# Tap products of a Hyena filter: high and low fp32r parts stacked on the summed index, two passes each, in place of whole fp32 factors

## The chip, the cores and the metric

The kernel runs on one core of one Trainium2 chip. The metric is the device time of the whole program in microseconds (us), where less is better. A time of the chip is the median of several runs; the profile is of one further execution, with its own time.

## The reference

The program is one layer of an encoder with two mixers side by side, run on a sample of 1024 positions and on a prompt of 256 positions. One mixer is grouped attention with rotary positions, the other is a Hyena operator: a long convolution whose filter a small network computes from the position. After them come an output projection, a gated feed-forward part and a final norm. What matters here is the filter:

```python
h = jnp.sin(fr * (z @ w1 + b1))          # (L, 64)
h = jnp.sin(fr * (h @ w2 + b2))          # (L, 64)
h = (h @ w3).reshape(L, N_DIRS, HY_WIDTH)   # (L, 2, 512): the taps
h = h * jnp.exp(-t[:, :, None] * jnp.abs(decay)[None])
...
return k / jnp.sum(jnp.abs(k), axis=0, keepdims=True)
```

`z` holds 33 position features and the hidden width is 64, so the product with `w3` sums over 64 terms. It is taken for both sequence lengths, forward and backward, over 512 channels.

## The kernel before

The program is written with a tile framework: pools hand out buffers by tag (a tag has a fixed number of slots), and the order of the instructions on each engine comes from a list scheduler that simulates the program while it is built, with its own estimates of the durations. Inside one engine the instructions run in that order.

The first part of the program projects the normed input onto the Hyena columns (`proj_hy`). It has 12 column tiles; each loads a 1024x128 weight block, splits it into an fp32r high part `wh` (a cast on ACT, line 498) and a low part `wl` (a subtraction on POOL, line 159), and multiplies it with the split input `ah`/`al`, three fp32r passes for each term (`mm3`, lines 166 to 168: high by high, low by high, high by low). The trace calls these products `us` (512 columns wide) and `up` (256 wide). ACT and DVE then apply a short convolution to the result `u`. The weight parts sit in the tag `w4`, which has 8 slots of 4 KB for each partition.

Interleaved with it runs `filter_stream`. It computes the two sine layers for 512 and 128 columns; the upper 64 partitions hold the second half of the positions, the lower 64 the first half. The results are `h2s` (in tag `s2`, 8 slots) for the sample and `h2p` (tag `s1`) for the prompt. Then `taps_of` runs four times, for the prompt's two halves of 256 channels (P0, P1) and the sample's two (S0, S1). It loads `w3` twice, into the lower and the upper partitions, and multiplies one 64-row slice of `h2` (128 positions) with the matching 64 rows of `w3` (512 columns: 256 channels in two directions) at line 352. There are 2 such products in each prompt half and 8 in each sample half. DVE multiplies each with an exponential from ACT (`h`, line 355), ACT and POOL gather the sums of magnitudes (`acc`), and DVE forms sums and differences (`e`, `q`). From these, further DVE work (`C`, `gaf`, `gtf`) and transform products (`fx`, line 281) make the filter's spectrum, which goes to DRAM. After the filter the main stream goes on with the query columns (`proj_att`), whose weights use `w4` too.

In the trace the tile names lose their digits: `f` is the tap product, `w` is `w3`. Line 159 is a helper that issues every elementwise two-input operation.

Of the kernel before, what the change touches and what calls it, by code (L numbers as in the profile page):

```python
# [12 lines left out]
F32R = mybir.dt.float32r  # L13
# [24 lines left out]
MUL, ADD, SUB = ALU.mult, ALU.add, ALU.subtract  # L38
# [62 lines left out]
def hymba_layer_kernel(ctx: ExitStack, tc: tile.TileContext, A, dbg=None):  # L101
    nc = tc.nc
    dbg = dbg or {}
    V, S, G, T, Q = nc.vector, nc.scalar, nc.gpsimd, nc.tensor, nc.sync
# [16 lines left out]
    def pool(tag, bufs, of=None):  # L121
        def make(name, shape, dt=F32):
            return (of or mem).tile([128] + list(shape), dt, name=name, tag=tag, bufs=bufs)
        return make


    w4, pf, u5 = pool("w4", 8), pool("pf", 10, res), pool("u5", 3)
    s2, r2, s1, fh = pool("s2", 8, mid), pool("r2", 3, mid), pool("s1", 5), pool("fh", 2, mid)
# [7 lines left out]
    def b1(name):  # L136
        return psm.tile([128, 512], F32, name=name, tag="b1", bufs=1)
# [11 lines left out]
    def bh(name):  # L149
        return psm.tile([128, 512], F32, name=name, tag="bh", bufs=2)  # L150

    def flat(t):
        return t.rearrange("p a b -> p (a b)")

    def stt(out, in0, scalar, in1, op0=MUL, op1=ADD, eng=None):
        (eng or V).scalar_tensor_tensor(out=out, in0=in0, scalar=scalar, in1=in1, op0=op0, op1=op1)

    def tt(out, in0, in1, op, eng=None):
        return (eng or V).tensor_tensor(out=out, in0=in0, in1=in1, op=op)  # L159

    def f(ap):
        return ap.bitcast(F32)
# [122 lines left out]
    def filter_stream():  # L285
# [11 lines left out]
        def sin_layer(ps, n, b, out):  # L297
            a = s2("sa", [512])[:, 0:n]
            V.tensor_scalar(out=a, in0=ps, scalar1=cols[:, b:b + 1], scalar2=cols[:, 58:59], op0=ADD, op1=MUL)
            k = s2("sk", [512])[:, 0:n]  # L300
            V.tensor_scalar(out=k, in0=a, scalar1=1.0 / (2 * math.pi), scalar2=MAGIC, op0=MUL, op1=ADD)
            V.tensor_scalar(out=k, in0=k, scalar1=MAGIC, scalar2=None, op0=SUB)
            for cw in CW:
                stt(a, k, -cw, a)
            V.tensor_scalar(out=a, in0=a, scalar1=PI_LO, scalar2=-PI_LO, op0=ALU.min, op1=ALU.max)
            S.activation(out=out, in_=a, func=AF.Sin)

        h2s = s2("h2s", [512])
        h2p = s1("h2p", [128])
        for n, off, h2 in ((512, 0, h2s), (128, 512, h2p)):  # L310
            p = b1("fp")
            T.matmul(out=p[:, 0:n], lhsT=w1bd, rhs=zf[0:66, off:off + n], start=True, stop=True)
            h1 = s2("h1", [512])[:, 0:n]
            with tc.issue_after(held[0].ins):
                sin_layer(p[:, 0:n], n, 56, h1)
            p = b1("fq")
            T.matmul(out=p[:, 0:n], lhsT=w2bd, rhs=h1, start=True, stop=True)
            sin_layer(p[:, 0:n], n, 57, h2)
            yield

        def taps_of(seq, hf, out):

            h2, na, toff = (h2s, 8, 0) if seq == "S" else (h2p, 2, 8)
            si = 0 if seq == "S" else 1
            nm = f"{seq}{hf}"
            cs = slice(hf * 256, (hf + 1) * 256)
            w3 = fh("w3", [2, 256])
            absd = fh("absd", [2, 256])
            for d in range(2):
                for h in range(2):  # L330
                    Q.dma_start(out=w3[h * 64:(h + 1) * 64, d],
                                in_=A["hy_f_w3"][0][:, d * HY + hf * 256:d * HY + (hf + 1) * 256])
                Q.dma_start(out=absd[:, d], in_=A["hy_decay"][0, d:d + 1, cs].broadcast_to([128, 256]))
            S.activation(out=absd, in_=absd, func=AF.Abs)
            acc = s2(f"acc{nm}", [512])
            if seq == "S":
                e, q = [], []
            else:
                e = [s2(f"e{nm}", [2, 256])]
                q = [s2(f"q{nm}", [2, 256])]  # L340
            half = na // 2
            for a2 in range(half):
                if seq == "S" and a2 % 2 == 0:
                    e.append(pf(f"e{a2 // 2}{nm}", [4, 256]))
                    q.append(pf(f"q{a2 // 2}{nm}", [4, 256]))
                h = pf(f"h{nm}", [2, 512])
                for i in range(2):
                    a = 2 * a2 + i
                    up = a >= half
                    p = bh("f3")  # L350
                    hs = slice(64, 128) if up else slice(0, 64)
                    T.matmul(out=p, lhsT=h2[hs, (a % half) * 128:(a % half) * 128 + 128],
                             rhs=flat(w3[hs]), start=True, stop=True)
                    S.activation(out=h[:, i], in_=flat(absd), func=AF.Exp, scale=negt[:, toff + a:toff + a + 1])
                    tt(h[:, i], p, h[:, i], MUL)
                    if a == 0:
                        V.memset(h[0:1, 0, 256:512], 0.0)
                        S.activation(out=acc, in_=h[:, i], func=AF.Abs)
                    else:
                        ab = s2("ab", [512])  # L360
                        S.activation(out=ab, in_=h[:, i], func=AF.Abs)
                        tt(acc, acc, ab, ADD, G)
                sl = slice(2 * (a2 % 2), 2 * (a2 % 2) + 2)
                tt(e[a2 // 2][:, sl], h[:, :, 0:256], h[:, :, 256:512], ADD)
                tt(q[a2 // 2][:, sl], h[:, :, 0:256], h[:, :, 256:512], SUB)
                if a2 < half - 1:
                    yield

            p = b1("fn")
            T.matmul(out=p[:, 0:256], lhsT=ones, rhs=acc[:, 0:256], start=True, stop=False)  # L370
            T.matmul(out=p[:, 0:256], lhsT=ones, rhs=acc[:, 256:512], start=False, stop=True)
            dn = s1(f"dn{nm}", [256])
            Q.dma_start(out=dn, in_=A["hy_d"][:, cs].broadcast_to([128, 256]))
            tt(dn, p[:, 0:256], dn, MUL)
            p = b1("fr")
            for c in range(2):
                for d in range(2):
                    T.matmul(out=p[:, 2 * c:2 * c + 2], lhsT=acc[:, d * 256 + c * 128:d * 256 + c * 128 + 128],
                             rhs=one, start=c == 0 and d == 0, stop=c == 1 and d == 1)
            nn = smh(f"nn{nm}", [2])  # L380
            V.tensor_scalar(out=nn, in0=p[:, 0:4:2], scalar1=float(na * 128), scalar2=None, op0=MUL)
            V.reciprocal(out=rn[:, si, 2 * hf:2 * hf + 2], in_=nn)
            V.tensor_scalar(out=rn2[:, si, 2 * hf:2 * hf + 2], in0=rn[:, si, 2 * hf:2 * hf + 2],
                            scalar1=RH, scalar2=None, op0=MUL)
            out.update(e=e, q=q, dn=dn)
            yield
# [16 lines left out]
        for hf in range(2):  # L403
            part = {}
            yield from taps_of("P", hf, part)
            for ri, nm in ((0, "e"), (1, "q")):
                g3 = two_point(part[nm][0], "f")
                for i in (0, 1):
                    one_set("P", hf, ri, 8 + i, g3, part["dn"], (512 * i, 256))
                yield  # L410
# [7 lines left out]

        parts = ({}, {})
        yield from taps_of("S", 0, parts[0])  # L420
        C = combined(parts[0]["e"], "S0")
        yield
        ahead = taps_of("S", 1, parts[1])
        for hf in range(2):
            for ri in range(2):
# [732 lines left out]
    held = []  # L1158
    first = startup()
    filt = filter_stream()  # L1160
    next(filt)

# [401 lines left out]
```

## Time and profile before

| what | us |
| --- | --- |
| runs on the chip | 1716.93, 1720.14, 1721.12 |
| their median | 1720.14 |
| the profiled execution's own time | 1717.49 |
| its span, first to last instruction | 1715.7 |
| TensorE busy in the span | 1627.2 |
| mean granted TensorE clock, share of full speed | 0.976 |

PE is TensorE's matmul, PEld its weight load, DVE is VectorE, ACT ScalarE, POOL GpSimd. A record of a matmul ends when its last column is through, so neighbouring records overlap; the distance from one start to the next is what a matmul costs the engine. A full fp32 matmul appears as two records.

### The profile page before, as it was taken

The numbers are of one execution on the slowest core, as the hardware profiler recorded it, in microseconds if no ns is written. First come the engines' busy times: TensorE is split into PE (matmuls) and PEld (weight loads), VectorE is DVE, ScalarE is ACT, GpSimd is POOL, SyncE is SP. The second block draws the span as 40 slices with busy tenths as digits, with TensorE's granted clock in tenths as the row PEclk, the third lists the DMA queues.
The fourth block names the chain that finished last, engine by engine and source line by source line (L and its number), as shares of the span: only waits on it lengthen the run. The fifth ranks groups of instructions, "written<-read, shape, count | busy, mean of one in ns | idle before, by whom it ended". The sixth has DMA issues, their size and how long they took to land.

```text
span 1715.7 us, 25792 instructions
## 1 busy us (share of the span) xinstructions
PE 1627.2 (95%) x9380; PEld 1456.4 (85%) x9380; DVE 990.4 (58%) x1512; ACT 689.4 (40%) x1332; POOL 924.3 (54%) x854
## 2 busy tenths in 40 slices
PE   6999999988998988999879999999999998999998
PEld 5777778987786876888769999999999998888886
DVE  5657779766756665556565444444444554554453
ACT  5434332345545557465352222222222222753341
POOL 6124343751437564352377776766677672663392
PEclk9999999998999999999989999999999999999999
DMA  6042333422232314334133444434344434875553
GB/s 213 29 135 87 115 117 123 141 92 62 88 96 69 101 53 140 137 120 151 50 105 96 149 136 152 136 124 132 108 130 140 147 108 176 293 253 173 172 185 122
DMA packets 175978, 221.12 MB, mean 129 GB/s; under 512 B 15344, under 2 KB 123560, under 8 KB 175851
## 3 DMA queue, kind: packets, MB, share of 16 engines
q1 hardware_dynamic: 175851, 219.47, 39.4%
q8 instruction: 74, 1.21, 0.3%
q14 instruction: 53, 0.43, 0.1%
HBM read 151.19 MB, written 68.22 MB: 128 GB/s over the span
## 4 chain that ended last, share of the span: by engine, by line
PE 85%; DVE 5%; DMA 3%; ACT 2%; POOL 2%; issue 1%; SPq 1%; DVEq 0%; POOLq 0%; ACTq 0%
PE prod L166 10%; PE prod L168 10%; PE prod L167 10%; PE dn L166 5%; PE dn L167 5%; PE dn L168 5%; PE ro L815 3%; PE s L773 3%; PE us L168 3%; PE us L167 3%; PE us L166 3%; PE pt L792 2%; PE fx L281 2%; PE xp L281 2%; PE hp L907 2%; PE wo L166 2%
## 5 line engine op out<-in xcount | busy, mean ns | idle before, releaser
L159 POOL TENSOR_TENSOR dbf<-dbr,dbf 128x512 fp32r<-128x512 f32 x77 | 107.7, 1400 | 114.2 <-ACT dbf L1426 111.0
L159 DVE TENSOR_TENSOR daf<-dar,daf 128x640 fp32r<-128x640 f32 x77 | 97.6, 1269 | 105.2 <-ACT daf L1426 104.6
L166 PE MATMUL dn<-dbf,daf 128*128 128x512 f32 x385 | 148.9, 393 | 4.8 <-ACT daf L1426 4.8
L167 PE MATMUL dn<-dbf,daf 128*128 128x512 f32 x385 | 149.3, 392 | 0.0
L168 PE MATMUL dn<-dbf,daf 128*128 128x512 f32 x385 | 147.6, 390 | 0.0
L159 DVE TENSOR_TENSOR vs<-prod,vs 128x256 f32<-128x256 f32 (+1 forms) x132 | 64.4, 488 | 79.4 <-PE prod L168 79.4
L792 PE MATMUL pt<-ident,P 128*128 128x128 f32 x544 | 81.3, 277 | 17.2 <-ACT PT L797 5.3
L777 DVE TENSOR_REDUCE nm<-s 128x1 f32<-128x1024 f32 (+1 forms) x68 | 82.5, 1215 | 18.0 <-PE s L773 16.4
L792 PEld LDWEIGHTS pt<-ident,P 128*128 128x128 f32 x544 | 64.9, 142 | 31.8 <-ACT PT L797 6.4
L166 PEld LDWEIGHTS dn<-dbf,daf 128*128 128x128 f32 x385 | 72.9, 190 | 20.2 <-ACT daf L1426 5.2
L159 POOL TENSOR_TENSOR wl<-wraw,wh 128x512 fp32r<-128x512 f32 x24 | 36.8, 1552 | 98.0 <-ACT wh L498 98.0
L781 ACT ACTIVATE P<-s,nm 128x1024 f32<-128x1024 f32 (+1 forms) x80 | 79.2, 996 | 23.2 <-DVE nm L777 22.9
L167 PEld LDWEIGHTS dn<-dbf,daf 128*128 128x128 f32 x385 | 73.0, 190 | 15.4
L1426 ACT CAST dbf<-dbr 128x512 fp32r<-128x512 f32 x77 | 47.8, 621 | 94.1 <-issue 42.5
L168 PEld LDWEIGHTS dn<-dbf,daf 128*128 128x128 f32 x385 | 72.6, 188 | 15.0
L167 PE MATMUL us<-al,wh 128*128 128x512 f32 (+1 forms) x208 | 82.9, 399 | 1.5 <-DVE al L159 1.5
L166 PE MATMUL us<-ah,wh 128*128 128x512 f32 (+1 forms) x208 | 82.0, 398 | 2.1 <-ACT ah L477 2.1
L168 PE MATMUL us<-ah,wl 128*128 128x512 f32 (+1 forms) x208 | 81.7, 393 | 0.0
L773 PE MATMUL s<-K,q2u 128*128 128x512 f32 x256 | 75.1, 424 | 2.3 <-DMA q2u<-q2d 1.7
L159 POOL TENSOR_TENSOR Y<-M 128x256 f32<-128x256 f32 x40 | 29.1, 741 | 84.9 <-DVE M L159 76.5
L1321 ACT CAST ws<-ws 128x512 fp32r<-128x512 f32 x44 | 27.2, 621 | 116.1 <-PE prod L168 81.7
L815 PE MATMUL ro<-PT,V 128*128 128x256 f32 x288 | 68.8, 391 | 3.4 <-ACT PT L797 1.7
(426 smaller groups left out, 5487.9 us busy)
## 6 DMA issues: line engine op xcount, KB each, us to landing
dar<-ads SPq DMA_DIRECT2D x44, 320.0 KB
a<-in_w_gate SPq DMA_DIRECT2D x44, 256.0 KB
a<-in_w_up SPq DMA_DIRECT2D x44, 256.0 KB
db<-in_w_down SPq DMA_DIRECT2D x88, 128.0 KB
dbr<-tdt SPq DMA_DIRECT2D x44, 256.0 KB
ads<-vx SPq DMA_DIRECT2D x33, 320.0 KB
dar<-ada SPq DMA_DIRECT2D x33, 320.0 KB
wraw<-in_w_in SPq DMA_DIRECT2D x36, 256.0 KB
```

What stands on the lines that cost most here:

```text
L159: return (eng or V).tensor_tensor(out=out, in0=in0, in1=in1, op=op)
L166: T.matmul(out=out, lhsT=lh, rhs=rh, start=first, stop=False)
L167: T.matmul(out=out, lhsT=lh, rhs=rl, start=False, stop=False)
L168: T.matmul(out=out, lhsT=ll, rhs=rh, start=False, stop=last)
L281: T.matmul(out=p[:, o * 256:(o + 1) * 256], lhsT=tab[:, j], rhs=g[:, c:c + 256], start=m == 0, stop=m == len(todo) - 1)
L773: T.matmul(out=s[:, c], lhsT=un["q2"][:, 0, bs], rhs=K2[kv, c][:, hl], start=hl == 0, stop=hl == 1)
L777: V.tensor_reduce(out=nm, in_=sf.rearrange("p (g k) -> p g k", g=n), axis=AX.X, op=ALU.max, negate=True)
L781: S.activation(out=P[:, ks], in_=sf[:, ks], func=AF.Exp, bias=nm[:, g:g + 1], accum_out=un["rs"][:, g, b:b + 1])
L792: T.transpose(out=pt[:, t * 128:(t + 1) * 128], in_=P[:, (t0 + t) * 128:(t0 + t + 1) * 128], identity=ident)
L815: T.matmul(out=o, lhsT=V1[0][:, t], rhs=PT[:, t0 + n], start=n == 0, stop=n == len(ts) - 1)
L907: T.matmul(out=p[:, c * 256:(c + 1) * 256], lhsT=y[:, a:a + 128], rhs=tab[:, t0:t0 + 256], start=m == 0, stop=m == len(todo) - 1)
L1426: S.copy(out=w[:, 0], in_=x)
```

## The change

After the second sine layer, the features are split. For each half of the positions, `H[:, z]` gets a tile of 128 partitions: its own 64 partitions take the rounded (fp32r) high part, the other 64 take the low part, value minus high part. So high and low parts lie one above the other along the index that the matmul sums over. `w3`, which already lies twice in the partitions, is split in `taps_of` into `wp[:, 0]` (high, cast on ACT) and `wp[:, 1]` (low, subtraction on POOL). Each tap product is then two fp32r matmuls over 128 rows that add up in one PSUM bank: (high and low of `H`) by high of `w3`, then by low of `w3`. `hs_` and `wp` take slots of the tag `w4`; `h2s` no longer holds one of `s2` for the length of the filter.

```diff
-        h2s = s2("h2s", [512])
-        h2p = s1("h2p", [128])
-        for n, off, h2 in ((512, 0, h2s), (128, 512, h2p)):
+        hs_ = w4("h2s", [2, 512], F32R)
+        hp_ = s1("h2p", [2, 128], F32R)
+        for n, off, H in ((512, 0, hs_), (128, 512, hp_)):
...
+            h2 = s2("h2", [512])[:, 0:n]
             sin_layer(p[:, 0:n], n, 57, h2)
+            for z, ps in enumerate((slice(0, 64), slice(64, 128))):
+                S.copy(out=H[ps, z], in_=h2[ps])
+                tt(h2[ps], h2[ps], f(H[ps, z]), SUB)
+            for z, ps, to in ((0, slice(0, 64), slice(64, 128)), (1, slice(64, 128), slice(0, 64))):
+                S.copy(out=H[to, z], in_=h2[ps])
             yield
...
+            wp = w4("w3p", [2, 512], F32R)
+            S.copy(out=wp[:, 0], in_=flat(w3))
+            tt(wp[:, 1], flat(w3), f(wp[:, 0]), SUB, G)
             S.activation(out=absd, in_=absd, func=AF.Abs)
...
-                    hs = slice(64, 128) if up else slice(0, 64)
-                    T.matmul(out=p, lhsT=h2[hs, (a % half) * 128:(a % half) * 128 + 128],
-                             rhs=flat(w3[hs]), start=True, stop=True)
+                    hc = H[:, int(up), (a % half) * 128:(a % half) * 128 + 128]
+                    T.matmul(out=p, lhsT=hc, rhs=wp[:, 0], start=True, stop=False)
+                    T.matmul(out=p, lhsT=hc, rhs=wp[:, 1], start=False, stop=True)
```

## Rows read from the trace of the kernel before

**Rows 1.** The page's first part: busy us, share of the span, instructions.
```profile
PE 1627.2 (95%) x9380; PEld 1456.4 (85%) x9380; DVE 990.4 (58%) x1512; ACT 689.4 (40%) x1332; POOL 924.3 (54%) x854
```
**Rows 2.** Windows: length, busy PE, PEld, DVE, ACT, POOL; clock, DMA share, GB/s.
```profile
65.00:115.00 50.00, 47.32 (x239) 38.55 (x239) 26.11 (x50) 20.02 (x34) 15.15 (x11) 0.97 0.39 118
115.00:150.00 35.00, 35.00 (x151) 24.85 (x150) 17.89 (x27) 11.64 (x21) 12.48 (x8) 1.00 0.30 88
150.00:195.00 45.00, 45.00 (x231) 37.51 (x230) 43.30 (x71) 17.31 (x28) 16.80 (x9) 1.00 0.30 90
195.00:245.00 50.00, 50.00 (x219) 36.24 (x218) 31.36 (x43) 18.39 (x31) 21.08 (x15) 1.00 0.35 109
245.00:294.00 49.00, 46.80 (x289) 42.80 (x288) 48.33 (x82) 13.95 (x25) 15.10 (x8) 0.97 0.43 135
```
**Rows 3.** The chain that ended last, 65 to 245 us: shares by line.
```profile
by line: PE us L168 19.5%; PE us L167 19.1%; PE us L166 19.0%; PE f L352 11.1%; PE fx L281 10.6%; PE up L168 5.5%; PE up L167 5.4%; PE up L166 5.3%; DMA tabf<-in_dft 1.5%; PE fr L378 1.3%; PE fn L370 0.7%; PE fn L371 0.7%; PE fq L317 0.1%; 
```
**Rows 4.** Line 352: count of records, ns min/median/max, first and last start us.
```profile
L352 PE MATMUL f<-w,h2s x32: 588/642/694, 131.0 to 241.2; 64*128 64x512 f32 x32
L352 PE MATMUL f<-w,h2p x8: 589/642/694, 86.1 to 112.7; 64*128 64x512 f32 x8
```
**Rows 5.** Timeline of PE around one tap product: start, us, instruction.
```profile
132.76 0.40 PE L167 MATMUL us<-al,wh 128*128 128x512 f32 x1
133.08 1.12 PE L352 MATMUL f<-w,h2s 64*128 64x512 f32 x2
134.14 0.50 PE L168 MATMUL us<-ah,wl 128*128 128x512 f32 x1
134.47 0.39 PE L166 MATMUL us<-ah,wh 128*128 128x512 f32 x1
...
134.94 0.40 PE L168 MATMUL us<-ah,wl 128*128 128x512 f32 x1
```
**Rows 6.** Timeline of PE around the two products of P0.
```profile
85.83 0.39 PE L168 MATMUL us<-ah,wl 128*128 128x512 f32 x1
86.15 1.13 PE L352 MATMUL f<-w,h2p 64*128 64x512 f32 x4
87.21 0.50 PE L166 MATMUL us<-ah,wh 128*128 128x512 f32 x1
87.54 0.28 PE L166 MATMUL up<-ah,wh 128*128 128x256 f32 x1
```
**Rows 7.** The split of the projection's weights: count, ns min/median/max, first and last start.
```profile
L498 ACT CAST wh<-wraw x24: 601/616/623, 6.5 to 189.7; 128x512 fp32r<-128x512 f32 x24
L159 POOL TENSOR_TENSOR wl<-wraw,wh x24: 1262/1302/2938, 7.4 to 192.8; 128x512 fp32r<-128x512 f32 x24
```
**Rows 8.** Groups on DVE, 65 to 300 us: busy, mean ns, idle before and releaser.
```profile
L159 DVE TENSOR_TENSOR hS<-f,hS 128x512 f32<-128x512 f32 x16 | 11.0, 690 | 21.7 <-PE f L352 20.0 <-ACT u L507 1.7
```
**Rows 9.** Timeline of ACT.
```profile
83.01 0.30 ACT L306 ACTIVATE h2p<-sa 128x128 f32<-128x128 f32 x1
...
84.62 1.34 ACT L354 ACTIVATE hP<-absd,negt 128x512 f32<-128x512 f32 x2
...
109.70 1.14 ACT L498 CAST wh<-wraw 128x512 fp32r<-128x512 f32 x2 [1.54 <-PE up L167]
```
**Rows 10.** Timeline of POOL.
```profile
82.20 2.56 POOL L159 TENSOR_TENSOR wl<-wraw,wh 128x512 fp32r<-128x512 f32 x2 [10.31 <-ACT wh L498]
84.72 2.93 POOL L159 TENSOR_TENSOR u<-u,u 128x1280 f32<-128x1280 f32 x1
...
261.18 4.51 POOL L159 TENSOR_TENSOR u<-u,u 128x1280 f32<-128x1280 f32 x1 [8.41 <-issue]
```
**Rows 11.** Timeline of DVE.
```profile
262.95 3.29 DVE L159 TENSOR_TENSOR gaf<-C1f,gtf 128x512 f32<-128x512 f32 x1
...
267.56 0.68 DVE L159 TENSOR_TENSOR gaf<-C3f,gtf 128x512 f32<-128x512 f32 x1
```
**Rows 12.** Timeline of PE at its one longer stop behind the taps.
```profile
266.34 1.10 PE L281 MATMUL fx<-gaf,tabf 128*128 128x256 f32 x4 [2.20 <-issue]
```

More of the change, by code (lines that the diff above doesn't have):

```diff
@@ L317, in filter_stream @@
             T.matmul(out=p[:, 0:n], lhsT=w2bd, rhs=h1, start=True, stop=True)
+            h2 = s2("h2", [512])[:, 0:n]
             sin_layer(p[:, 0:n], n, 57, h2)
+            for z, ps in enumerate((slice(0, 64), slice(64, 128))):
[3 more added lines that the diff above has]
+                S.copy(out=H[to, z], in_=h2[ps])
             yield
         def taps_of(seq, hf, out):
-            h2, na, toff = (h2s, 8, 0) if seq == "S" else (h2p, 2, 8)
+            H, na, toff = (hs_, 8, 0) if seq == "S" else (hp_, 2, 8)
             si = 0 if seq == "S" else 1
```

## The prediction

> **What bounds the kernel now.** I read the page's shares first: TensorE is busy for 1627.2 us, 95% of the span, and the next engine for 58% [rows 1]. That is an average, so I cut out the stage of the change, 65 to 294 us, in windows. From 115 to 245 us PE is busy in every microsecond, at a granted clock of 1.00; just before, it has 47.32 of 50 us, just after, 46.80 of 49 [rows 2]. The second column to watch is DVE: it has slack at first (26.11 of 50 and 17.89 of 35), but 43.30 of 45 from 150 to 195 and 48.33 of 49 from 245 to 294. POOL and ACT are below half everywhere. Then the chain: from 65 to 245 us it runs over PE nearly all the way, and line 352, the tap product, has 11.1% of it [rows 3], about 20 us. DVE says the same from its side: it waited 20.0 us for `f` before its multiplications `hS` [rows 8]. So in this stage PE's own time sets the pace, and a microsecond taken from PE should move everything behind it, until DVE has no slack left.
>
> **What a tap product costs now.** By the code there are 20 of them, and the trace has 32 and 8 records, two for each [rows 4]. The record's 1.12 us is not the whole cost, since PE also changes over to it and back. I measure start to start. From 132.76 to 134.47 us PE does one `us` pass, the tap product and another `us` pass: 1.71 us. Two `us` passes in a row, 134.47 to 134.94, take 0.47 us. The tap product therefore costs 1.71 - 0.47 = 1.24 us [rows 5]. P0 is an exception: its two products use different halves of the partitions, stand side by side, and together take 87.54 - 85.83 - 0.47 = 1.24 us, as long as one [rows 6]. The other 18 stand alone in the trace. In all 19 x 1.24 = 23.6 us of PE.
>
> **What it costs afterwards.** Forty fp32r passes with 128 rows and 512 columns. The trace has this very shape in `us`: 0.235 us from start to start, half of the 0.47 above, and the weight load runs beside it. The bounds are this 0.235 us and the 0.40 us of the record if a pass overlapped with nothing [rows 5]: 40 x 0.235 = 9.4 us or 40 x 0.40 = 16.0 us. I take 9.4, because the neighbours are fp32r passes of the same kind, so that nothing is left to change over. PE saves 23.6 - 9.4 = 14.2 us; at the other bound, 7.6 us.
>
> **What is added elsewhere.** On ACT: four copies of 512 columns, four of 128, and four casts for `wp`. With 0.616 us for a cast of 512 columns [rows 7] and 0.30 us for 128 columns [rows 9] that is 8 x 0.616 + 4 x 0.30 = 6.1 us, in 180 us in which ACT is busy about a third of the time [rows 2]. On DVE: four subtractions, at most 4 x 0.69 = 2.8 us [rows 8], all before P0, where DVE has 24 us free [rows 2]. On POOL: four subtractions at 1.30 us (up to 2.94), 5.2 us [rows 7] (up to 11.8). I cost all of these at nothing on the path; what hides them is the projection's `us` and `up` passes, which need none of it. Without that cover the prompt's features would be late: `h2p` is ready at 83.31 and the first taps run at 86.15 [rows 6, 9]; two copies and a subtraction in a row add about 1 us, up to 2 with ACT's exponential in between. Behind the first tap in PE's queue stand only projection passes, so a wait there costs its own length once.
>
> `hs_` and `wp` take two of `w4`'s eight slots. That matters because the slots are short today: the cast for a later weight tile at 109.70 us had waited 1.54 us for the `up` pass that freed its slot [rows 9]. With eight slots four tiles are in hand, so three remain for PE to work on while a new one is loaded; with six slots two remain. One tile has at least 48 passes of 512 columns, 48 x 0.235 = 11.3 us, and two have 22.6. A load needs 1.14 us on ACT and 2.56 us on POOL [rows 9, 10] once its data is there. I cost it at nothing; with no tile in hand it would be 3.7 us for each tile. `s2` gains a slot, which I also cost at nothing. No DMA is added.
>
> **Where the saving may leak.** DVE does not get shorter. From 245 to 294 us it has no slack, and PE stopped there for 2.20 us until 266.34, right behind `gaf` on DVE, which ended at 262.95 + 3.29 = 266.24 [rows 11, 12]. If PE comes to this place earlier, such stops get likelier. I charge one more of them, 2.2 us; the bounds are none (or this one gone, since the order moves) and what the first rival gives.
>
> **The sum.** The span of 1715.7 us becomes 1715.7 - 14.2 + 2.2 = 1703.7. The profiled execution lasted 1717.49 us, 1.8 more than its span, so its like would take 1705.5. It was 2.65 us faster than the median of the runs, 1720.14; set on that median, the forecast is 1720.1 - 12.0 = 1708.1, say 1708.
>
> **First rival: DVE becomes the bound from 150 us on.** For it: 43.30 of 45 and 48.33 of 49 us. Against it: from 195 to 245 DVE has 18.6 us free [rows 2], and much of that is waiting for `f` itself. If it is so, only what is saved before 150 us counts: 10 products in 9 places, 9 x 1.24 - 20 x 0.235 = 6.5 us. POOL's added subtractions can make it worse. An addition of 512 columns on DVE takes 0.68 us alone, but 3.29 us while POOL's `u` ran from 261.18 to 265.69 and it ended 0.55 us after that [rows 10, 11]. Two of the four new subtractions on POOL come after 150 us: 2 x 1.30 = 2.6 us of DVE. That gives 1720.1 - 6.5 + 2.6 = 1716.2, between 1713 and 1719.
> The Trainium skill ("SBUF — State Buffer", section "SBUF: two separate sides") has a rule for this: GpSimd and a VectorE instruction with two SBUF inputs share a port pair as an exclusive lock, and the later one waits for the whole instruction of the other. By that rule, the trace agrees: the DVE row ended only after POOL's.
>
> **Second rival: the passes don't fold in.** If each pass costs its record's 0.40 us, PE saves 7.6 us and the time is 1720.1 - 7.6 + 2.2 = 1714.7. Against it speaks every run of `us` passes at 0.235 us.
>
> **Third rival, on the other side: PE waits for POOL at each half.** The second pass of a half's first tap needs `wp`'s low part. POOL works in order, and 2.56 us of weight splits and 2.93 us of `u` can stand ahead [rows 10]; with its own 1.30 us that is 6.8 us. If PE's order puts the tap ahead of projection passes that could run, PE stands still: four halves give 27 us, less the 14.2 saved and without the extra stop, 1720 + 13 = 1733 us. It decides where the stop is over 3.6 us for each half. For it: the order is made by a simulation whose durations are not the chip's. Against it: the order now puts the tap late enough that PE is busy 100% from 115 to 245 us [rows 2].
>
> **Chances.** A measurement of this kernel can tell about 0.3%, 5.2 us, from no change, so faster means below 1715.0 and slower above 1725.3. The forecast, with times from 1703 to 1713, has 0.71; the first rival 0.16, the second 0.05, the third 0.06; 0.02 is for none of them. Faster: 0.71, a third of the first rival and half of the second, 0.78. Slower: 0.07. Same: 0.15. The range reaches down to the full saving with the stop at 266 us gone as well, 1720.1 - 14.2 - 2.2 = 1703.7, less some 2.5 us by which runs differ: 1701. It reaches up to the end of the first rival, 1719.
>
> **What would show it.** In the profile after, line 352's records should be gone and 40 records with 128 rows and 512 columns stand in their place, 0.235 us from start to start among `us` passes. The transform products that follow the stop at 266.34 us [rows 12] should come about 12 us earlier, and that distance should last to the end. DVE's wait for `f` (20.0 us) should shrink by more than half. If the first rival holds, PE shows more stops between 150 and 294 us, released by DVE; if the third, PE stops before the first tap of each half, released by POOL. The prediction is wrong in the main if PE's gain is there after these transform products and lost later, which no row here prepares for: then a different order of the later streams has eaten it.

## The result, and the profile after

The changed kernel takes 1731.6 us (median of 4 runs, 1731.19 to 1732.75), the kernel before 1718.54 (1716.56 to 1721.12) beside it: ratio 1.0070, interval 1.0054 to 1.0086. It is slower by 12 to 13 us, where 12 us less were forecast, and lies above the range. The first part of its page, against [rows 1]:

```profile
span 1729.5 us, 25826 instructions
...
PE 1618.0 (94%) x9380; PEld 1461.2 (84%) x9380; DVE 1005.8 (58%) x1516; ACT 698.3 (40%) x1346; POOL 924.4 (53%) x858
```

PE is busy 9.2 us less and the span is 13.8 us longer, so PE stands still 23 us more. The windows of [rows 2], of the kernel after:

```profile
65.00:115.00 50.00, 35.24 (x169) 30.11 (x168) 29.61 (x49) 25.30 (x43) 17.93 (x12) 0.83 0.36 107
115.00:150.00 35.00, 35.00 (x182) 30.07 (x181) 21.74 (x31) 17.12 (x29) 13.10 (x10) 1.00 0.29 88
150.00:195.00 45.00, 41.27 (x201) 34.38 (x200) 44.93 (x65) 13.35 (x21) 17.49 (x11) 0.96 0.33 104
195.00:245.00 50.00, 50.00 (x255) 42.79 (x254) 39.17 (x50) 22.91 (x40) 27.39 (x19) 1.00 0.44 137
245.00:294.00 49.00, 46.67 (x258) 40.88 (x258) 48.86 (x83) 12.87 (x22) 10.29 (x6) 0.97 0.43 135
```

The first window has 35.24 us of PE, where it had 47.32, and its clock is at 0.83, not 0.97. In the later windows little is lost but 3.7 us in the third. PE's timeline in the first window shows the stops (in brackets: the idle time before the row, and what ended it):

```profile
67.11 0.28 PE L168 MATMUL up<-ah,wl 128*128 128x256 f32 x1
72.70 0.55 PE L166 MATMUL up<-ah,wh 128*128 128x256 f32 x1 [5.30 <-ACT h2s L325]
...
77.11 0.39 PE L318 MATMUL fq<-h,wbd 128*128 128x128 f32 x2
84.65 0.79 PE L166 MATMUL us<-ah,wh 128*128 128x512 f32 x1 [7.15 <-ACT wh L508]
...
88.60 0.79 PE L362 MATMUL f<-w3p,h2p 128*128 128x512 f32 x1 [2.30 <-ACT h2p L325]
89.19 0.63 PE L363 MATMUL f<-w3p,h2p 128*128 128x512 f32 x1
89.61 0.63 PE L362 MATMUL f<-w3p,h2p 128*128 128x512 f32 x1
```

Three stops, 14.75 us. From 84.65 to 93.0 us a pass of 512 columns costs 0.42 us from start to start (89.19 to 89.61), not 0.23; after the first stop, to 76 us, a pass of 256 columns costs 0.21 us, not 0.12. Two windows over the work behind the stops (after):

```profile
72.70:76.00 3.30, 3.30 (x15) 3.30 (x16) 1.38 (x4) 1.82 (x4) 0.00 (x0) 0.50 0.25 71
84.60:92.00 7.40, 5.05 (x12) 3.89 (x13) 3.03 (x6) 4.75 (x10) 3.34 (x3) 0.50 0.55 186
```

The granted clock there is 0.50, the lower of the two levels, 1.2 GHz. With the 1.0 us from 92 to 93, 3.30 + 5.05 + 1.0 = 9.35 us of PE's work ran at half speed, which cost some 4.7 us more than at full speed.

The passes themselves came as forecast. Timeline of PE around a tap product, to be held against [rows 5], and the count of the two lines:

```profile
132.96 0.39 PE L167 MATMUL us<-al,wh 128*128 128x512 f32 x1
133.19 0.39 PE L362 MATMUL f<-w3p,h2s 128*128 128x512 f32 x1
133.41 0.39 PE L363 MATMUL f<-w3p,h2s 128*128 128x512 f32 x1
133.64 0.39 PE L168 MATMUL us<-ah,wl 128*128 128x512 f32 x1
```

```profile
L362 PE MATMUL f<-w3p,h2s x16: 389/392/397, 131.6 to 235.7; 128*128 128x512 f32 x16
L363 PE MATMUL f<-w3p,h2s x16: 389/392/398, 131.8 to 235.9; 128*128 128x512 f32 x16
```

A tap product takes 133.64 - 133.19 = 0.45 us where it took 1.24.

**Where the first stops come from.** The first two stand before passes of the projection, not before tap products. Casts on ACT, in the kernel after:

```profile
17.47 0.61 ACT L508 CAST wh<-wraw 128x512 fp32r<-128x512 f32 x1
...
68.15 1.25 ACT L322 CAST h2s<-h 64x512 fp32r<-64x512 f32 x2
69.42 0.62 ACT L342 CAST w3p<-w 128x512 fp32r<-128x512 f32 x1
...
83.46 0.62 ACT L342 CAST w3p<-w 128x512 fp32r<-128x512 f32 x1 [4.64 <-DMA w<-in_hy_f_w]
83.98 0.61 ACT L508 CAST wh<-wraw 128x512 fp32r<-128x512 f32 x1
```

and in the kernel before:

```profile
17.52 0.61 ACT L498 CAST wh<-wraw 128x512 fp32r<-128x512 f32 x1
31.05 0.62 ACT L498 CAST wh<-wraw 128x512 fp32r<-128x512 f32 x1 [0.81 <-DMA wraw<-in_w_in]
32.42 1.14 ACT L498 CAST wh<-wraw 128x512 fp32r<-128x512 f32 x2
36.57 0.62 ACT L498 CAST wh<-wraw 128x512 fp32r<-128x512 f32 x1 [3.00 <-DMA wraw<-in_w_in]
```

Before, the weights of the third and fourth tile are cast from 31 to 37 us. After, no weight is cast between 17.47 and 83.98 us, though ACT is free and SP has issued the third tile's loads early. SP's queue, after:

```profile
28.16 0.93 SPq L507 DMA_DIRECT2D wraw<-in_w_in  x2
...
78.40 1.11 SPq L338 DMA_DIRECT2D w<-in_hy_f_w  x2
```

The order of the casts, `h2s`, `w3p`, `w3p`, `wh`, is the order in which the program asks the tag `w4` for slots. `hs_` is asked for early and first written at 68 us, after two sine layers; `w3p` of P0 comes next. P1's `w3p` waits besides for its data: the slot that P0's `w` gives back at 71.4 us, when it is split, goes to P0's `absd` first, and P1's `w` is loaded at 78.40, right behind the exponentials that read `absd` (they end at 78.37). The third tile's weights stand behind all of them. From 67 us on PE has only the second tile's `up` passes left, for which the one buffer of `up` is not free yet, and no third tile.

### The profile page after: what moved, and what is told of

It reads as the page before. It is cut to its first block, busy times and chain, and to the rows that moved or that the text cites. A ratio compares the mean times of both kernels' runs of the same rounds, so it can differ in the third digit from the quotient of the medians.

```text
span 1729.5 us, 25826 instructions
## 1 busy us (share of the span) xinstructions
PE 1618.0 (94%) x9380; PEld 1461.2 (84%) x9380; DVE 1005.8 (58%) x1516; ACT 698.3 (40%) x1346; POOL 924.4 (53%) x858
## 4 chain that ended last, share of the span: by engine, by line
PE 69%; DVE 4%; POOL 4%; ACT 2%; issue 1%; DMA 1%; SPq 0%; POOLq 0%; DVEq 0%; ACTq 0%
PE prod L166 10%; PE prod L168 10%; PE prod L167 10%; PE dn L166 5%; PE dn L167 5%; PE dn L168 5%; PE s L783 3%; PE ro L825 3%; PE pt L802 2%; PE wo L166 2%; PE wo L168 2%; PE wo L167 2%; PE xp L281 2%; PE ro L829 2%; PE hp L917 2%
## 5 line engine op out<-in xcount | busy, mean ns | idle before, releaser
L159 POOL TENSOR_TENSOR ws<-ws,ws 128x512 fp32r<-128x512 f32 x44 | 57.2, 1300 | 22.0 <-ACT ws L1331 22.0
```

## The experiments

Each kernel ran beside the kernel before on its chip (1720.0 to 1720.1 us, 13 to 21 runs, beside e1 to e10). Two positions in the trace split the span: the first key transposition (`qt<-ident,kk`, right behind the projection of the query columns) and the first product of the feed-forward part (`prod`). "Order" says what share of PE's instructions from the first attention score to `prod`, named by their tiles, stands in the same sequence as in the kernel before (1.00 is the same sequence; the expectations below have other counts of this, with the same grouping). The split is that of one execution: e9's took 3.2 us and e8's 2.3 us more than the kernel's median, those of e3, e6 and e10 1.9 to 2.5 us less, and that of before 1.0 us less than 1718.5 (2.5 us less than the later medians). So a difference of 2 or 3 us between two rows of these columns shows nothing by itself.

| kernel | time (runs) | ratio, interval | first `kk` | `kk` to `prod` | rest of span | order |
| --- | --- | --- | --- | --- | --- | --- |
| before | 1718.5 (4) | 1 | 373.05 | 515.6 | 827.0 | 1.00 |
| after | 1731.6 (4) | 1.0070 [1.0054, 1.0086] | 379.70 | 522.7 | 827.1 | 0.49 |
| e1, nothing in `w4` | 1710.6 (5) | 0.9950 [0.9932, 0.9968] | 360.89 | 520.7 | 827.0 | 0.49 |
| e2, slots without the products | 1744.9 (4) | 1.0145 [1.0128, 1.0162] | 392.97 | 522.3 | 826.9 | 0.49 |
| e3, loads first | 1714.5 (6) | 0.9968 [0.9953, 0.9982] | 365.64 | 518.0 | 827.3 | 0.96 |
| e4, six slots | 1721.4 (10) | 1.0006 [0.9997, 1.0016] | 373.52 | 516.9 | 828.5 | 1.00 |
| e5, e1 and e3 | 1710.4 (5) | 0.9942 [0.9930, 0.9955] | 363.86 | 516.2 | 828.5 | 1.00 |
| e6, only H in `w4` | 1718.8 (9) | 0.9997 [0.9987, 1.0008] | 361.31 | 526.2 | 827.1 | 0.51 |
| e7, only `w3p` in `w4` | 1705.9 (3) | 0.9919 [0.9904, 0.9934] | 358.94 | 517.7 | 827.3 | 1.00 |
| e8, after, other order | 1724.2 (11) | 1.0027 [1.0018, 1.0036] | 379.45 | 517.1 | 828.1 | 0.99 |
| e9, before, other order | 1722.4 (10) | 1.0012 [1.0000, 1.0023] | 375.39 | 521.3 | 827.3 | 0.49 |
| e10, e1, order of before | 1705.5 (4) | 0.9920 [0.9905, 0.9935] | 359.09 | 513.8 | 828.3 | 0.99 |

**e1: the change with nothing in `w4`.** H becomes two tiles of `s2`, the parts of `w3` two more.

```diff
-        hs_ = w4("h2s", [2, 512], F32R)
+        hs_ = [s2(f"h2s{z}", [512], F32R) for z in range(2)]
...
-            wp = w4("w3p", [2, 512], F32R)
+            w3h = s2("w3h", [512], F32R)
+            w3l = s2("w3l", [512], F32R)
```

> The change with its parts H and w3p kept in the tag s2 instead of w4; the arithmetic and the instructions are those of the change. Theory 1 (the tag w4 hands out its slots in the order of the program, so the weights of column tile 2 queue behind h2s and two w3p whose writers are late, and PE runs out of weights between 67 and 89 us): the stops of 5.3, 7.2 and 2.3 us are gone, the span up to the first attention score is 8 to 14 us shorter than before's 394.0 us, and the time is 1704 to 1713 us unless the attention part is reordered for the worse. Theory 3 (the added copies and subtractions themselves make PE wait): stops of together about 15 us stay between 65 and 115 us, and the time is 1725 us or more.

The first window of e1:

```profile
65.00:115.00 50.00, 50.00 (x265) 43.04 (x265) 30.07 (x52) 25.29 (x47) 18.25 (x13) 1.00 0.42 127
```

PE has no stop left there, with all of the added work on ACT, DVE and POOL still in it, and the first key transposition comes 12.2 us before that of the kernel before. The added work is hidden, as forecast; the place of its results was what cost.

**e2: the old products with the two slots of the change.** `h2s` and a copy of `w3` lie in `w4`; the products, and everything else, are those of before.

```diff
-        h2s = s2("h2s", [512])
+        h2s = w4("h2s", [2, 512])[:, 0]
...
+            wp = w4("w3p", [2, 512])
+            S.copy(out=wp[:, 0], in_=flat(w3))
...
-                             rhs=flat(w3[hs]), start=True, stop=True)
+                             rhs=wp[hs, 0], start=True, stop=True)
```

> The kernel before, whole fp32 products, but with h2s and a copy of w3 (one cast on ACT for each half) in the tag w4, as the change has them. Theory 1: PE stops for about 12 to 15 us between 65 and 115 us as in the change, nothing is saved on the products, and the time is 1730 to 1742 us. Theory 3: within 4 us of the kernel before, since no part is split and no pass is added.

Its longest waits of PE, 60 to 115 us (us in all, times, longest):

```profile
PE us L166 <- ACT wh L500: 4.4, 1, 4.4
PE up L166 <- DVE u L156: 3.7, 1, 3.7
PE f L354 <- ACT h2p L306: 1.7, 1, 1.7
```

The slots alone, without one fp32r tap, bring the three stops back, 9.8 us, and cost 19.9 us up to the first key transposition. The stops are shorter than expected and the time is above the range expected: work at the lower clock (0.83 in the window from 65 to 115 us, as after the change) and a wait of 3.85 us at 171.57 come on top.

**e3: the change, with the third and fourth tile's weights asked for ahead of the filter's tiles.**

```diff
+        for t in order[2:4]:
+            early[t] = load(t)
+        yield
...
-                W, ps[t] = load(t), b2("us")
+                W, ps[t] = early.get(t) or load(t), b2("us")
```

> The change with one thing moved: the weight loads of column tiles 2 and 3 are traced ahead of the filter's tiles, so that they stand first in the tag's order; the number of slots and of their users is unchanged. Theory 1: the stops before 89 us go, as in the run with the parts in s2; time 1704 to 1714 us. Theory 2 (eight slots with three of them held are simply too few): later tiles' weights come late instead, PE stops behind ACT's weight cast elsewhere before 260 us, and the time stays above 1722 us.

PE is busy for 46.70 us of the first window, and the first key transposition is at 365.64, 14.1 us earlier than in the changed kernel, with both tenants still in `w4`: only the order of asking was moved. The 3.3 us that PE still waits in this window (0.80, 0.31, 1.26 and 0.87) are all before transform products `fx`, none before a projection pass. The time, 1714.5, is half a microsecond above the range expected.

**e4: the kernel before with two slots of `w4` held from the start until the last half of the filter.**

```diff
+    kept = [w4(f"kept{i}", [8]) for i in range(2)]
+    for t in kept:
+        V.memset(t, 0.0)
```

> The kernel before with two of the eight w4 slots taken early by two small tiles and held until the last filter half; nothing else is changed. Theory 1: six slots are enough, as the weights are asked for in good time; within 4 us of the kernel before, 1715 to 1723 us. Theory 2: PE waits for weight casts and the time rises by 8 us or more.

1.0006: six slots in place of eight cost nothing that can be measured. The change can hold a third (`hs_` and two `w3p`); e3 holds the same three and has its weights in time. A lack of slots is not the cause.

**e5 to e8** take the two causes apart: which of the two tenants of `w4` blocks, and what the order of the attention part is worth.

e5 joins the edits of e1 and e3.

> The change with nothing in `w4`: H as two `s2` tiles and w3's high and low parts as two `s2` tiles, and besides the loads of the third and fourth weight tiles traced ahead of the filter's tiles, which brings the order of the attention part's TensorE instructions back to that of the kernel before. If the loss had two causes, the place in `w4` (6.9 us before the first attention score) and the other order of the attention part (6.8 us), both are gone: first score at 382 to 385 us, attention part 495 to 497 us, time 1704 to 1709 us, ratio 0.991 to 0.994. If the order of the attention part is worth nothing by itself and the first run's longer attention part has another cause, that part stays at 500 us and the time at 1710 us or more.

The order is that of before, and `kk` to `prod` went back from 520.7 to 516.2 us; but the first key transposition came 3 us later than in e1 (PE has 45.92 of 50 us in the first window; 2.8 of the 4.1 us missing are waits for `h2p`), so the time is e1's, above the range expected.

e6 has `hs_` in `w4` and the parts of `w3` in `s2` (the second half of e1's diff).

> The change with `hs_` alone in `w4`; w3's high and low parts lie in `s2`. If the slots of `w4` are given out in program order, `hs_`, first written near 68 us, still holds back the weights of the third tile, but no `w3p` stands between them any more: the first of these weights is cast near 69 us instead of 84 us, and TensorE stops for 3 to 6 us near 67 to 72 us and hardly at all from 77 to 85 us; first score near 386 to 390 us. The attention part has the slower order (0.80 like the kernel before), 499 to 501 us, so 1713 to 1719 us. If it is `w3p` that holds the weights back, the third tile's weights come in time and TensorE doesn't stop before 80 us: first score at 382 us.

ACT and PE in e6:

```profile
67.58 1.25 ACT L322 CAST h2s<-h 64x512 fp32r<-64x512 f32 x2
68.85 1.66 ACT L509 CAST wh<-wraw 128x512 fp32r<-128x512 f32 x3
```

```profile
69.52 0.50 PE L166 MATMUL us<-ah,wh 128*128 128x512 f32 x1 [2.70 <-ACT wh L509]
```

The third tile's weights are cast right behind `h2s`, 15 us earlier than after the change, and PE stops for 2.70 us and once more for 0.31 (and 1.10 us for `h2p`). The first key transposition is at 361.31, only 0.4 us behind e1's. Nearly all of that gain is lost behind it: `kk` to `prod` takes 526.2 us, 5 us more than in e1, more than expected.

e7 has `w3p` in `w4` and H in `s2` (the first half of e1's diff).

> The change with `w3p` alone in `w4`; H lies in `s2`. The data of the first half's w3 is there at 24 us, so if slots go out in program order and only a late first writer hurts, `w3p` is cast near 30 us, and the weights of the third tile are cast right behind it, before 45 us: no stop of more than 1 us between 65 and 85 us, first score at 382 to 386 us. Only the second half's `w3p`, whose data came at 78 to 80 us in the changed kernel, can hold a tile back then; if its loads stay that late, the third tile's weights come at 84 us again and the stops are those of the changed kernel. The order of the attention part is that of the kernel before, 495 to 497 us; time 1704 to 1710 us, or 1719 to 1724 us with the stops.

ACT in e7:

```profile
28.57 0.60 ACT L343 CAST w3p<-w 128x512 fp32r<-128x512 f32 x1
42.89 0.62 ACT L343 CAST w3p<-w 128x512 fp32r<-128x512 f32 x1
43.41 1.14 ACT L509 CAST wh<-wraw 128x512 fp32r<-128x512 f32 x2
```

`w3p` stands ahead of the third tile in the same tag as after the change, but nothing stands ahead of `w3p`: it is written at 28.57, its raw data's slot goes to `absd` (32.20) and the next one to P1's `w` (37.76), P1's `w3p` follows at 42.89, and the third tile's weights behind it, all before PE needs them. The first key transposition is at 358.94, 14.1 us before that of the kernel before.

So neither tenant costs much by itself. The first key transposition is at 360.89 with none of them in `w4` (e1), 361.31 with `hs_` alone, 358.94 with `w3p` alone, and 379.70 with both. `hs_`, with its late first writer, starts the delay and puts the third tile's weights off to 68.85; that is nearly in time. Only with `w3p` behind it, whose second half gets its data after the first half has been written and used, do they come at 83.98. In all of these kernels the first writes come in the order of asking; by what step the framework makes them so is not shown.

e8 is the changed kernel with one constant of the order of work at another value.

```diff
-    MS = 16
+    MS = 14
```

> The changed kernel with one constant of its order of work, MS, at 14 and not 16. The filter and the projection keep their order, the attention part gets one like that of the kernel before (0.994). If the order is what the 6.8 us of the attention part are paid for, the first score stays near 401 us with the same stops before it, the attention part takes 495 to 498 us instead of 501.5, and the time is 1723 to 1728 us. If the attention part is longer because of the change's arithmetic or of the stops before it, it stays at 500 to 502 us and the time at 1731 us.

The first key transposition stays (379.45), and `kk` to `prod` falls from 522.7 to 517.1 us. The expected split by the first score did not hold, because the order moved some key transpositions behind the first scores, which now come at 394.7; the time, 1724.2, is as expected. PE's longest waits from 300 to 870 us, after:

```profile
PE ro L825 <- ACT PT L807: 7.6, 2, 6.9
PE qt L676 <- ACT kk L659: 6.7, 2, 3.7
...
PE pt L802 <- DVE ya L159: 6.3, 2, 6.0
```

and in e8:

```profile
PE ro L829 <- DVE PT L159: 7.7, 4, 4.7
...
PE pt L802 <- DVE ya L159: 3.7, 2, 2.6
...
PE qt L676 <- ACT kk L659: 2.8, 2, 1.4
```

The single waits of 6.9 and 6.0 us are gone with the order; one of 4.7 us has come.

**e9 and e10: the order by itself**, on kernels without the stops. e9 is the kernel before with MS at 15, e10 is e1 with MS at 14.

> The kernel before, with nothing of the change, and the constant MS of its order of work at 15 and not 16. Up to the first attention score its TensorE order is that of before (0.999 alike), from there to the feed-forward part it is like that of the run with H alone in `w4` (0.957) and not like before (0.549). If the order by itself has a price, the first key transposition stays near 373 us, and from it to the feed-forward part it takes 521 to 527 us instead of 515.6: 1725 to 1731 us. If the longer attention part came with the change and not with the order, the time is that of before, 1717 to 1722 us.

> The first run's kernel (nothing of the change in `w4`) with MS at 14: the order up to the first score is the same (0.998), the attention part has the order of the kernel before (0.994). If the order has a price, the first key transposition stays at 361 us, from it to the feed-forward part it takes 515 to 518 us instead of 520.7, and the time is 1704 to 1708 us, 3 to 6 us under the first run. If it has none, 1709 to 1711 us.

In e9's trace `kk` to `prod` takes 521.3 us, 5.7 more than before, as expected of the order; but its runs are only 0.12% slower (2 us; 0 to 4), less than the 5 us expected. The traced execution of e9 lies 3.2 us above its kernel's median and that of before 1.0 to 2.5 below, so much of the 5.7 us need not be the order's. e10 is 5 us faster than e1 (0.9920 against 0.9950), as expected. By the runs the order has a price of 2 to 7 us, not the same in each place, and in e9 its interval begins at nothing.

## Why the prediction was wrong

**What held.** The rate: 0.23 us for a pass, no changing over, as the sum's 9.4 us for forty of them wanted. The saving: 14.2 us less the 2.2 charged, 12.0, stands against 12.2 us at the first key transposition in e1, 14.1 in e7 and 14.0 in e10. The nearness of e1 is in part luck: the charge was for one more stop at the transform products near 266 us, which came in none of the three. From 65 to 294 us PE stands still for 4.88 us before, 6.86 in e1, 5.37 in e7 and 5.40 in e10; e1 pays about as much as was charged, but from 150 to 196 us. The added work on ACT, DVE and POOL: hidden under projection passes, as e1's full window shows. Only the wait for `h2p`, priced at 1 to 2 us and costed at nothing, was there after the change, 2.30 us; in e1 and e7 it is gone, in e6 it is 1.10 and in e5 2.8 us. With both causes of loss removed, e7 and e10 take 0.8% less than before, 1705.9 and 1705.5 us: where the forecast was, and 2 us better. In e7 the filter's last transform products start at 299.7 us, 12.2 before those of the kernel before (311.9), which is the sign that the prediction named; after the change they start at 307.8.

**The step that failed** is the paragraph on `w4`. It counted slots: six in place of eight, two tiles in hand in place of three, "I cost it at nothing". The count costs nothing, as it said (e4). What it left out is that the tag gives its slots out in the order in which the program asks, so that a slot given to a tile with a late first writer holds up every later asker, however early its data is there. Its price, "with no tile in hand 3.7 us for each tile", was thought of as a load's length; the wait ran to the end of the two sine layers at 68 us and, through the two `w3p`, to 84 us. e1 and e3 remove it by the place and by the order of asking, e2 brings it without the change, e6 and e7 show that it takes both tenants: the one with the late writer, and the one that passes the delay on and lengthens it.

Up to the first key transposition the account is: 14.75 us of stops, less the 2.7 us that PE had waited in this window before, 4.7 us for the work at the lower clock, 3.7 us missing in 150 to 195 us, less 14.2 saved, makes about 6.3; the traces are 6.65 us apart.

**The second step** is the last sentence, which named a different order of the later streams as what "no row here prepares for". It happened, in part: `kk` to `prod` took 7.1 us more in the trace, though after the change only 4 of the 12 us were there at the last transform products. The four kernels made of two places and two orders give its share of the ratio:

| | order as after | order like before |
| --- | --- | --- |
| `hs_`, `wp` in `w4` | 1.0070 (after) | 1.0027 (e8) |
| in `s2` | 0.9950 (e1) | 0.9920 (e10) |

The place is worth 1.1 to 1.2%, 18 to 21 us; the order 0.3 to 0.4%, 5 to 7 us. The place alone, put right (e1), brings most of what was forecast; the order alone (e8) leaves the kernel slower than before. The part of the order isn't settled to a microsecond: in e9 it was worth 2 us, and e6's order, much like e9's (0.94 by the same count), took 526.2 us for the part where e9's took 521.3. Why the scheduler turns to the one or the other was not tried.

**The first rival** (DVE as the bound) was there in part. From 150 to 195 us DVE is busy for 44.93 of 45 us and PE has 41.27; PE's longest stop there (after):

```profile
PE fr L388 <- DVE dnS L159: 3.0, 1, 3.0
```

e2, which saves nothing on the products, waits 3.85 us at 171.57 before the same `fr` product, so this stop goes with the place in `w4` and not with PE's being faster. e1 has 41.05 there as well, e7 45.00, with DVE busy for 43.54 and 44.85 of 45 us: a DVE near its full share doesn't by itself stop PE. The stops of e1 from 150 to 196 us are released by DVE (4.5 us, the longest 1.4), as the rival said, and cost it part of the saving; e7 has none of them. From 245 to 294 us little moved: one stop of 2.20 us before [rows 12], one of 2.33 after. DVE's wait for `f`, 20.0 us [rows 8], was to shrink by more than half; it is 14.3 us after and 11.4 in e7, so that was too much.

**The second rival** (passes that don't fold in) is refuted by the 0.23 us. **The third** had the right sign and the wrong mechanism: neither after the change nor in e1 did PE wait for POOL before a tap product for more than 0.23 us, and the long stops were before projection passes.

Two readings in the prediction are off without touching the sum. The 24 us in which DVE is free are those of the whole window from 65 to 115 us; before the first tap at 86 us DVE had 10.8 free. And after the change all four of POOL's new subtractions come before 133 us, none of them after 150.

One row of after bears on what the first rival said of DVE and POOL. DVE's subtraction for `h2s` and POOL's for `w3p` met:

```profile
70.23 1.72 DVE L159 TENSOR_TENSOR h<-h,h2s 64x512 f32<-64x512 f32 x1
...
72.08 0.47 DVE L156 SCALAR_TENSOR_TENSOR u<-up,cols,u 128x255 f32<-128x255 f32 x1
72.58 0.69 DVE L159 TENSOR_TENSOR h<-h,h2s 64x512 f32<-64x512 f32 x1
```

```profile
70.12 1.28 POOL L159 TENSOR_TENSOR w3p<-w,w3p 128x512 fp32r<-128x512 f32 x1 [36.85 <-ACT w3p L342]
```

The same subtraction takes 1.72 us beside POOL's, ending at 71.95, 0.55 us after it, and 0.69 us alone. Behind it stood the step on `up` that ended at 72.55, and PE went on at 72.70: the profile names `h2s` for this stop, but by the code PE's next pass needs only the one buffer of `up`, and by the times it was that; PE was left waiting for it because it had no other tile to work on. By these rows the meeting cost about 1 us here. By the rule of the Trainium skill ("SBUF — State Buffer", section "SBUF: two separate sides") GpSimd and a VectorE instruction with two SBUF inputs share a port pair as an exclusive lock; the trace agrees.

## What to carry to other kernels

Where buffers come from a pool by tag, ask of each new tenant who asks behind it and when its own first writer runs, not only how many slots remain: a tile that is written late belongs in a tag whose later askers are later still. Look as well at what stands between it and the tile that PE needs: here a second tenant, harmless by itself, made a delay to 69 us one to 84 us. Where the order is made by a planner, hold the order of the parts that were not touched against the one before, and compare kernels of the same order, before a difference of a few us is put down to the edit. And where PE stops for as long as here, look at the granted clock of the work behind the stop and price that work by it.

## What was not expected of the hardware

After stops of 5.30 and 7.15 us PE's next work ran at a granted clock of 0.50, in 72.70 to 76.00 and in 84.60 to 93.0 us, with 0.42 us for a pass of 512 columns that otherwise takes 0.23. Some 15 us of stops so cost about 4.7 us more than their length.
